# Four of eight K-tile pairs of the FFN inputs by Strassen's scheme, with two sets of blocks for their sums and two sums formed by accumulating DMA

## The chip, the core and the metric

The kernel runs on one core of one Trainium2 chip. The core has a matrix engine (TensorE, in the profile PE, with its weight loads as PEld), VectorE (DVE), ScalarE (ACT), GpSimd (POOL) and SyncE (SP); 128 partitions of on-chip memory (SBUF); a matrix accumulator (PSUM) of eight banks; and 16 DMA engines that move data between device memory (HBM) and SBUF. Each engine works through its own queue in order and waits on semaphores. The metric is the device time of one execution in microseconds; less is better.

## The reference

One layer of a streaming encoder on 256 tokens of width 2048, all in float32. Cut to what matters here:

```python
def swiglu_ffn(x, w_in, w_out):
    g, u = jnp.split(x @ w_in, 2, axis=-1)
    return (jax.nn.silu(g) * u) @ w_out
...
        h = layer_norm(ALPHA * h + 0.5 * swiglu_ffn(h, ffn1_w_in[l], ffn1_w_out[l]), ln_ffn1_g[l], ln_ffn1_b[l])
        mix = hybrid_mixer(h, w_in[l], gate_bias[l], rel_bias[l], q_a_norm[l], w_q_b[l], kv_a_norm[l],
                           w_kv_b[l], w_o_a[l], w_o_b[l], w_out[l], cos, sin)
        h = layer_norm(ALPHA * h + mix, ln_mix_g[l], ln_mix_b[l])
        xa = memory_cross_attention(h, mem, mem_ln_g[l], mem_ln_b[l], w_xq[l], w_xkv[l], w_xo[l])
        h = layer_norm(ALPHA * h + xa, ln_x_g[l], ln_x_b[l])
        h = layer_norm(ALPHA * h + 0.5 * swiglu_ffn(h, ffn2_w_in[l], ffn2_w_out[l]), ln_ffn2_g[l], ln_ffn2_b[l])
```

The change touches the product `x @ w_in` of both FFNs: (256 x 2048) by (2048 x 11008), where 5504 columns are the gate g and 5504 the "up" half u.

## The kernel before

**Halves.** A float32 product is made of three products of a shorter format (float32r). Every operand v is kept as a high half (v rounded, a copy by ScalarE) and a low half (v minus the high half, a subtraction by VectorE). A product of x and w is x_hi w_hi + x_hi w_lo + x_lo w_hi: three matmuls, "passes", into one bank. `split` (L244, L245) makes both halves; `run` does the same for weights in L213 and L216.

**Weights.** All weights stream from HBM as tiles of 128 x 2048 into `raw` (three buffers, DMAs issued by SP in L175), and their halves go into units of 128 x 1024 (`unit`, four buffers each for high and low halves). `run` walks through a list of items, each with its weights, and emits the loading of the next item's weights (`load`, at most four units in use) ahead of the item's matmuls. Each item may have a priority. A framework then orders the instructions of every engine's queue and sets the semaphores.

**The FFN's input.** The 5504 gate and up columns are taken in groups of 512 (`in_group`, j = 0 to 9, and a rest of 384, j = 10). A group needs four banks: two token halves (tt) by gate and up (g). Its K dimension of 2048 is 16 tiles of 128, taken as eight pairs k; each pair is one weight tile of 1 MiB. A plain pair (`mm_pair`, L296) issues 2 tiles x 2 x 2 x 3 = 24 matmuls of 512 columns. Group 0 of FFN 1 stands in `start`, and group 0 of FFN 2 in `first_group`. The hidden columns are processed in three parts (`F_SPLIT`: groups 0 to 2, 3 to 6, 7 to 10); after each part its output product (`out_proj`, L285) follows, four columns of the output by three or four weight tiles.

**Strassen's scheme.** Seen as a 2 x 2 by 2 x 2 block product (two K tiles, two token halves, gate and up), a pair can be computed with seven block products rather than eight: 21 matmuls (`mm_sums`, L340). In groups 1 to 9 the pairs in `SUMS_AT` (k = 2, 4, 6) are done so. The sums on the activations' side are made once per FFN (`sum_forms`, L311 to L317, into blocks X0, X1). The sums on the weights' side are made for each such pair from the raw tile (`form_sums`, L183): three additions on VectorE into a block H5 (one of 1024 columns, two of 512), then the halves of the two sums of 1024 columns each, into blocks that rotate over X2, X3 and H4. Beside them the pair's plain blocks are split (1024 and 512 columns). Four products go to a second set of four banks (`qs`), which serve as the next group's banks afterwards; `shared` (L568 to L573) takes them out after the last Strassen pair, and `product` in `hidden` (L614 to L617) adds them to the group's banks. `turn` transposes the gated result (L629) into the blocks H0 to H3; in the middle of a part it runs inside the next group, between its second and third pair.

**Order of emission.** In `load(i)`: fetch tile i, form the sums of tile i and tile i + 1 if they are Strassen pairs, then split tile i.

## Time and profile before

| | us |
|---|---|
| median of 3 runs (2529.89 to 2531.62) | 2531.01 |
| the profiled execution | 2530.41 |
| its span, first to last instruction | 2528.6 |

The page of the profile gives the busy time of each engine over the span; the chain that ended last, followed back from the last instruction to what released each step; groups of instructions by source line (L296 is line 296); and the DMA queues. A row of a group names the operation, output and inputs by the program's names, the shape, the count, then busy time, mean ns of one, and the idle time in front of them with what ended it. Windows give the busy time of each engine in a stretch of the span. Matmuls overlap in their pipeline, so a single one is listed with 389 ns while the next starts before it ends.

### The profile page before, as it was taken

To read this page: it belongs to the slowest core of one execution; us is meant where nothing else is said; L and a number is where in the kernel's file an instruction comes from. 1 tells how busy PE (TensorE), PEld (TensorE's weight loads), DVE (VectorE), ACT (ScalarE), POOL (GpSimd) and SP (SyncE) were. 2 spreads that over 40 slices of the span, in tenths; PEclk is the share of its full clock that TensorE was granted. 3 is DMA by queue.
4 is the path that set the end of the run, shared out by engine and by line. 5 is a ranking of instruction groups with operands and counts; after the bars stand their busy time and mean duration, and the time that the engine had idled before them with its cause. 6 is when DMAs were issued, how large, how long until landed. Compare 5 with 4: busy or idle time off the path is not lost.

```text
span 2528.6 us, 32077 instructions
## 1 busy us (share of the span) xinstructions
PE 2512.6 (99%) x12590; PEld 2123.7 (84%) x12590; DVE 1808.0 (72%) x2420; ACT 1279.3 (51%) x1734; POOL 30.0 (1%) x87
## 2 busy tenths in 40 slices
PE   9999999999999999999999999999999999999998
PEld 8888888889888888888888888888888888888896
DVE  6967985796666776755558784555878788758856
ACT  5545553554444555544445554454555455445543
POOL 0000000000000000000000000000000000000000
PEclk9999999999999999999999999999999999999999
DMA  7655655555645644555457565544555655555563
GB/s 259 243 186 183 216 193 192 198 200 191 227 155 185 201 143 142 183 192 183 175 192 261 188 217 194 189 163 138 200 181 202 211 205 183 203 197 200 183 231 136
DMA packets 74040, 488.04 MB, mean 193 GB/s; under 512 B 8609, under 2 KB 8865, under 8 KB 20769
## 3 DMA queue, kind: packets, MB, share of 16 engines
q1 hardware_dynamic: 69216, 468.18, 52.9%
q0 software_dynamic: 3808, 15.73, 2.0%
q8 instruction: 98, 1.61, 0.2%
q10 hardware_dynamic: 864, 2.10, 0.2%
q14 instruction: 54, 0.43, 0.1%
HBM read 482.69 MB, written 2.10 MB: 192 GB/s over the span
## 4 chain that ended last, share of the span: by engine, by line
PE 96%; DVE 2%; DMA 1%; ACT 0%; issue 0%; DVEq 0%; ACTq 0%
PE mm L285 31%; PE mm L265 17%; PE mm L296 13%; PE at L296 10%; PE mm L266 8%; PE mm L340 5%; PE at L340 5%; PE mm L254 2%; DMA raw<-ffn_w_in 1%; PE at L717 1%; DVE lo L216 0%; PE at L1152 0%; PE at L1130 0%; PE at L863 0%; PE at L391 0%; PE at L928 0%
## 5 line engine op out<-in xcount | busy, mean ns | idle before, releaser
L216 DVE TENSOR_TENSOR lo<-raw,hi 128x1024 fp32r<-128x1024 f32 (+1 forms) x742 | 893.7, 1208 | 576.1 <-ACT hi L213 561.5
L213 ACT CAST hi<-raw 128x1024 fp32r<-128x1024 f32 (+1 forms) x742 | 769.9, 1039 | 917.5 <-PE mm L285 369.1
L285 PE MATMUL mm<-hi,H 128*128 128x512 f32 x1640 | 508.7, 389 | 0.0
L265 PE MATMUL mm<-T,hi 128*128 128x512 f32 x1168 | 415.3, 399 | 0.0
L285 PEld LDWEIGHTS mm<-hi,H 128*128 128x128 f32 x1640 | 307.9, 188 | 63.4
L266 PE MATMUL mm<-T,lo 128*128 128x256 f32 x1168 | 328.2, 281 | 0.0
L285 PE MATMUL mm<-lo,H 128*128 128x512 f32 x820 | 319.2, 389 | 0.0
L296 PE MATMUL mm<-hi,T 128*128 128x512 f32 (+1 forms) x1024 | 308.7, 376 | 0.4 <-ACT hi L244 0.4
L265 PEld LDWEIGHTS mm<-T,hi 128*128 128x128 f32 x1168 | 219.5, 188 | 54.3 <-issue 1.2
L296 PE MATMUL at<-hi,T 128*128 128x512 f32 x800 | 253.0, 389 | 0.0
L265 PE MATMUL mm<-H,hi 128*128 128x512 f32 x640 | 225.9, 397 | 0.0
L266 PEld LDWEIGHTS mm<-T,lo 128*128 128x128 f32 x1168 | 220.6, 189 | 0.1
L296 PEld LDWEIGHTS mm<-hi,T 128*128 128x128 f32 x1024 | 190.4, 188 | 31.1 <-ACT hi L244 1.4
L296 PE MATMUL mm<-lo,T 128*128 128x512 f32 (+1 forms) x512 | 193.1, 377 | 0.2 <-DVE lo L245 0.2
L285 PEld LDWEIGHTS mm<-lo,H 128*128 128x128 f32 x820 | 154.0, 188 | 31.9 <-DVE lo L216 0.2
L266 PE MATMUL mm<-H,lo 128*128 128x256 f32 x640 | 179.0, 280 | 0.0
L296 PEld LDWEIGHTS at<-hi,T 128*128 128x128 f32 x800 | 150.2, 188 | 31.2
L296 PE MATMUL at<-lo,T 128*128 128x512 f32 x400 | 156.1, 390 | 0.0
L265 PEld LDWEIGHTS mm<-H,hi 128*128 128x128 f32 x640 | 120.2, 188 | 29.0
L285 PE MATMUL mm<-hi,X 128*128 128x512 f32 x416 | 130.0, 390 | 0.0
L245 DVE TENSOR_TENSOR lo<-raw,hi 128x1024 fp32r<-128x1024 f32 (+1 forms) x126 | 119.2, 975 | 10.3 <-ACT hi L244 10.1
L244 ACT CAST hi<-raw 128x1024 fp32r<-128x1024 f32 (+1 forms) x126 | 103.7, 853 | 44.3 <-PE mm L296 13.3
(242 smaller groups left out, 3181.7 us busy)
## 6 DMA issues: line engine op xcount, KB each, us to landing
raw<-ffn_w_in SPq DMA_DIRECT2D x151, 1024.0 KB, 4.8
raw<-ffn_w_out SPq DMA_DIRECT2D x80, 1024.0 KB, 4.8
raw<-w_gate SPq DMA_DIRECT2D x32, 1024.0 KB, 4.8
raw<-w_qk SPq DMA_DIRECT2D x16, 1024.0 KB, 4.8
raw<-w_o_b SPq DMA_DIRECT2D x16, 1024.0 KB, 4.8
raw<-w_out SPq DMA_DIRECT2D x16, 1024.0 KB, 4.9
raw<-w_xk SPq DMA_DIRECT2D x16, 1024.0 KB, 4.8
raw<-w_xv SPq DMA_DIRECT2D x16, 1024.0 KB, 4.9
```

The lines of the kernel that those rows point to most:

```text
L213: self.nc.scalar.copy(hi[:, :m], raw[:, c:c + m])
L216: self.nc.vector.tensor_tensor(lo[:, :m], raw[:, c:c + m], hi[:, :m].bitcast(F32), ALU.subtract)
L244: self.nc.scalar.copy(hi, src)
L245: self.nc.vector.tensor_tensor(lo, src, hi.bitcast(F32), ALU.subtract)
L254: self.nc.tensor.matmul(ps, w[u][wi][:, c:c + P], x.at(xi, kt), start=(j == 0 and k == 0), stop=(j == n - 1 and k == 2),)
L265: self.nc.tensor.matmul(ps, hi, x.both(kt), start=(kt == 0), stop=False)
L266: self.last_mm = self.nc.tensor.matmul(ps[:, :S], lo, x.at(0, kt), start=False, stop=(kt == n - 1))
L285: self.last_mm = self.nc.tensor.matmul(ps, x.at(xi, kt)[:, tt * P:(tt + 1) * P], w[u][wi][:, c:c + 512], start=(start and j == 0 and k == ...
L296: self.last_mm = self.nc.tensor.matmul(ps[tt, g][:, :n], x.at(xi, kt)[:, tt * P:(tt + 1) * P], hi_lo[wi][:, g * n:(g + 1) * n], start=(kt ...
L340: self.last_mm = self.nc.tensor.matmul(bank, a[xi], hi_lo[wi][:, c:c + 512], start=own and first and j == 0, stop=own and last and j == 2)
L717: self.nc.tensor.transpose(ps[:, i * P:(i + 1) * P], s[:, c:c + P], self.ident)
```

## The change

- `SUMS_AT` goes from (2, 4, 6) to (2, 3, 5, 6): four pairs of each group of 512 go by Strassen's scheme. The layout of the weights in HBM swaps gate and up in both K tiles of such a pair, so that the three plain blocks lie side by side.
- The two blocks of sums on the weights' side each have a whole set for high and low halves: (X2, X3) and (H4, H5), used in turn.
- For the first two Strassen pairs of a group (`ADDED`), the first sum of 1024 columns is not made by VectorE. GpSimd copies 1024 columns from HBM into a buffer Y0 or Y1 and then adds 512 columns, twice, in a second, accumulating DMA from HBM. It is emitted up to four items ahead. VectorE makes the other two sums of 512 from it (into Y2). In the other two pairs VectorE makes all three.
- The units for weight halves become two rings (`place`) of 4 x 1024 columns; weights of the FFN inputs get one subtraction for their whole low half (2048, or 1536 in a Strassen pair).
- In `mm_pair` and `mm_sums` all matmuls with high halves of the weights come first, then those with low halves.
- In `load(i)` the split of tile i comes ahead of the sums.
- The scratch space for GpSimd's DMA descriptors is set to 4096 bytes.

```diff
--- before.py
+++ after.py
@@ -23,8 +23,9 @@
 NF = D_FF // P
 NG = D_FF // 512
 F_SPLIT = (12, 16, 15)
-SUMS_AT = (2, 4, 6)
-SUM_TAGS = ("X2", "X3", "H4")
+SUMS_AT = (2, 3, 5, 6)
+ADDED = (0, 1)
+SETS = (("X2", "X3"), ("H4", "H5"))
 A_HEADS, A_DIM = 16, 64
 B_HEADS, NOPE, ROPE, V_DIM = 16, 128, 64, 128
 X_HEADS, X_DIM = 4, 512
...
@@ -102,6 +102,8 @@
         self.uid = 0
         self.chain = None
         self.turns = 0
+        self.cur = 0
+        self.ring = [self.halves.tile([P, UNITS * 1024], F32R, name=f"ring{i}") for i in range(2)]
 
 
     def name(self, s):
@@ -166,7 +168,7 @@
                 return 2
             return 0 if w[1] else -(-w[0].shape[1] // 1024)
 
-        raws, sums = {}, {}
+        raws, sums, adds = {}, {}, {}
 
         def fetch(i):
             if i not in raws:
@@ -175,46 +177,72 @@
                 self.last_load = self.nc.sync.dma_start(raws[i][:, :ap.shape[1]], ap)
             return raws[i]
 
+        def four(ap, a=4):
+            return ap.rearrange("p (a n) -> p a n", a=a)
+
+        def begin_sums(i):
+            ap, k = queue[i].ap, self.turns % 2
+            self.turns += 1
+            t = self.block(f"Y{k}", (P, 1024))
+            adds[i] = t, k
+            if queue[i].added:
+                self.nc.gpsimd.dma_start(t, ap[:, 512:1536])
+                self.nc.gpsimd.dma_start(four(t, 2), four(ap)[:, 0:1].to_broadcast([P, 2, 512]), accum_op=ALU.add)
+
         def form_sums(i):
-            raw, t = fetch(i), self.block("H5", (P, 2048))
-            for a, b, c in ((slice(0, 1024), raw[:, 0:1024], raw[:, 512:1536]),
-                            (slice(1024, 1536), t[:, 0:512], raw[:, 1024:1536]),
-                            (slice(1536, 2048), t[:, 1024:1536], raw[:, 1536:2048])):
-                self.nc.vector.tensor_tensor(t[:, a], b, c, ALU.add)
-            sums[i] = []
-            for k in range(2):
-                blk = self.block(SUM_TAGS[self.turns % len(SUM_TAGS)], (P, 2, 1024), F32R)
-                self.turns += 1
-                self.split(t[:, k * 1024:(k + 1) * 1024], blk[:, 0, :], blk[:, 1, :])
-                sums[i].append((blk[:, 0, :], blk[:, 1, :]))
+            r = four(fetch(i))
+            if i not in adds:
+                begin_sums(i)
+            (t, k), u = adds[i], self.block("Y2", (P, 1024))
+            if not queue[i].added:
+                self.nc.vector.tensor_tensor(four(t, 2), r[:, 1:3], r[:, 0:1].to_broadcast([P, 2, 512]), ALU.add)
+            for out, a, b in ((u[:, :512], t[:, :512], 2), (u[:, 512:], u[:, :512], 3)):
+                self.nc.vector.tensor_tensor(out, a, r[:, b], ALU.add)
+            hi, lo = (self.block(g, (P, 2048), F32R) for g in SETS[k])
+            for src, c in ((t, 0), (u, 1024)):
+                self.split(src, hi[:, c:c + 1024], lo[:, c:c + 1024])
+            sums[i] = [(four(hi)[:, a], four(lo)[:, a]) for a in range(4)]
 
         def load(i):
             w = queue[i]
             raw = fetch(i)
+            for k in range(i, min(i + 5, len(queue))):
+                if isinstance(queue[k], Sums) and queue[k].added and k not in adds:
+                    begin_sums(k)
+            got = split_own(i, w, raw)
 
             for k in (i, i + 1):
                 if k < len(queue) and isinstance(queue[k], Sums) and k not in sums:
                     form_sums(k)
-            got = []
+            return got + sums[i] if isinstance(w, Sums) else got
+
+        def split_own(i, w, raw):
             if isinstance(w, Sums):
-                for a, b in ((1024, 2048), (0, 512)):
-                    hi, lo = self.unit()
-                    self.split(raw[:, a:b], hi[:, :b - a], lo[:, :b - a])
-                    got.append((hi, lo))
-                return got + sums[i]
+                hi, lo = self.place(1536)
+                for a, b in ((0, 512), (512, 1536)):
+                    self.nc.scalar.copy(hi[:, a:b], raw[:, 512 + a:512 + b])
+                self.nc.vector.tensor_tensor(lo, raw[:, 512:], hi.bitcast(F32), ALU.subtract)
+                return [(hi[:, c:c + 512], lo[:, c:c + 512]) for c in (0, 512, 1024)]
             ap, tags = w
             n = ap.shape[1]
+            step = 768 if ap.tensor.name.endswith("_w_in_r") else 1024
             if tags:
-                blk = [self.block(g, (P, 2048), F32R) for g in tags[:2]]
-            step = 768 if ap.tensor.name.endswith("_w_in_r") else 1024
+                hi, lo = [self.block(g, (P, 2048), F32R) for g in tags[:2]]
+            elif "_w_in" in ap.tensor.name:
+                hi, lo = self.place(n)
+                for c in range(0, n, step):
+                    self.nc.scalar.copy(hi[:, c:c + step], raw[:, c:c + step])
+                self.nc.vector.tensor_tensor(lo, raw[:, :n], hi.bitcast(F32), ALU.subtract)
+                return [(hi[:, c:c + step], lo[:, c:c + step]) for c in range(0, n, step)]
+            got = []
             for c in range(0, n, step):
                 m = min(step, n - c)
-                hi, lo = [x[:, c:c + step] for x in blk] if tags else self.unit()
-                self.nc.scalar.copy(hi[:, :m], raw[:, c:c + m])
+                h, l = [x[:, c:c + m] for x in (hi, lo)] if tags else self.place(m)
+                self.nc.scalar.copy(h, raw[:, c:c + m])
 
                 with self.tc.issue_after(self.chain.ins) if self.chain is not None else nullcontext():
-                    self.nc.vector.tensor_tensor(lo[:, :m], raw[:, c:c + m], hi[:, :m].bitcast(F32), ALU.subtract)
-                got.append((hi, lo))
+                    self.nc.vector.tensor_tensor(l, raw[:, c:c + m], h.bitcast(F32), ALU.subtract)
+                got.append((h, l))
             return got
 
         def early(w):
@@ -289,15 +317,16 @@
 
     def mm_pair(self, ps, w, n, x, kts):
 
-        for (hi_lo, kt) in zip(w, kts):
-            for tt in range(2):
-                for g in range(2):
-                    for k, (wi, xi) in enumerate(((0, 0), (1, 0), (0, 1))):
-                        self.last_mm = self.nc.tensor.matmul(
-                            ps[tt, g][:, :n], x.at(xi, kt)[:, tt * P:(tt + 1) * P],
-                            hi_lo[wi][:, g * n:(g + 1) * n],
-                            start=(kt == 0 and k == 0), stop=(kt == KT - 1 and k == 2),
-                        )
+        for passes in (((0, 0), (0, 1)), ((1, 0),)):
+            for (hi_lo, kt) in zip(w, kts):
+                for tt in range(2):
+                    for g in range(2):
+                        for wi, xi in passes:
+                            self.last_mm = self.nc.tensor.matmul(
+                                ps[tt, g][:, :n], x.at(xi, kt)[:, tt * P:(tt + 1) * P],
+                                hi_lo[wi][:, g * n:(g + 1) * n],
+                                start=(kt == 0 and wi + xi == 0), stop=(kt == KT - 1 and wi == 1),
+                            )
 
     def sum_forms(self, x):
 
@@ -321,25 +350,22 @@
 
 
         k = 2 * SUMS_AT[i]
-        u1, u2, t13, t24 = w
+        r0, r2, r3, t0, t1, t2, t3 = w
 
         def plain(kt, tt):
             return [x.at(a, kt)[:, tt * P:(tt + 1) * P] for a in (0, 1)]
 
         n5, s2, n3, s3 = ([forms[i][:, a, j, :] for a in (0, 1)] for j in range(4))
         first, last = i == 0, i == len(SUMS_AT) - 1
-        for bank, a, (hi_lo, c), own in (
-                (ps[0, 0], plain(k + 1, 0), (u1, 512), False),
-                (ps[0, 1], n3, (u1, 0), False),
-                (qs[0], plain(k, 0), (u2, 0), True),
-                (qs[1], n5, (t13, 0), True),
-                (qs[3], s3, (t13, 512), True),
-                (qs[2], s2, (t24, 0), True),
-                (ps[1, 0], plain(k + 1, 1), (t24, 512), False)):
-            for j, (wi, xi) in enumerate(((0, 0), (1, 0), (0, 1))):
-                self.last_mm = self.nc.tensor.matmul(
-                    bank, a[xi], hi_lo[wi][:, c:c + 512],
-                    start=own and first and j == 0, stop=own and last and j == 2)
+        parts = ((ps[0, 0], plain(k + 1, 0), r3, False), (ps[0, 1], n3, r2, False), (qs[0], plain(k, 0), r0, True),
+                 (qs[1], n5, t0, True), (qs[3], s3, t1, True), (qs[2], s2, t2, True),
+                 (ps[1, 0], plain(k + 1, 1), t3, False))
+        for passes in (((0, 0), (0, 1)), ((1, 0),)):
+            for bank, a, hi_lo, own in parts:
+                for wi, xi in passes:
+                    self.last_mm = self.nc.tensor.matmul(
+                        bank, a[xi], hi_lo[wi],
+                        start=own and first and wi + xi == 0, stop=own and last and wi == 1)
 
 
     def rsqrt(self, v, y, a):
...
@@ -493,9 +519,11 @@
     def raw_tile(self):
         return self.wraw.tile([P, 2048], F32, tag="raw", name=self.name("raw"))
 
-    def unit(self):
-        return (self.whi.tile([P, 1024], F32R, tag="hi", name=self.name("hi")),
-                self.wlo.tile([P, 1024], F32R, tag="lo", name=self.name("lo")))
+    def place(self, n):
+        c, k = self.cur, -(-n // 1024)
+        assert c + k <= UNITS
+        self.cur = (c + k) % UNITS
+        return [r[:, c * 1024:c * 1024 + n] for r in self.ring]
 
 
     def ffn(self, tag, xT, st, first=None, steps=None, late=None, before=None, tags=None):
@@ -550,7 +578,7 @@
                     if i == 0:
                         qs.update((a, self.group_tile(j + 1)) for a in range(4))
                     self.mm_sums(ps, qs, w, xT(), self.forms, i)
-                self.add(fn, Sums(ap))
+                self.add(fn, Sums(ap, i in ADDED))
                 if i == len(SUMS_AT) - 1:
                     self.add(lambda: self.shared(qs), prio=SOON)
                 continue
@@ -1249,7 +1277,7 @@
     w = np.stack([m.reshape(k // P, P, c // n, n) for m in (u, g)])
     if n == 512:
         for i in SUMS_AT:
-            w[:, 2 * i + 1, :, 1:] = w[::-1, 2 * i + 1, :, 1:].copy()
+            w[:, 2 * i:2 * i + 2, :, 1:] = w[::-1, 2 * i:2 * i + 2, :, 1:].copy()
     return w.transpose(3, 2, 1, 0, 4).reshape(c // n, P, k // P * 2 * n)
 
 
@@ -1314,7 +1342,7 @@
     from concourse.bass_utils import run_bass_kernel_spmd
 
     arrays = _layout(inputs)
-    nc = bacc.Bacc("TRN2", target_bir_lowering=False, num_devices=1)
+    nc = bacc.Bacc("TRN2", target_bir_lowering=False, num_devices=1, dynamic_dma_scratch_size=4096)
     t = {
         k: nc.dram_tensor(k, v.shape, mybir.dt.from_np(v.dtype), kind="ExternalInput").ap()
         for k, v in arrays.items()
```

In `start` the two units of a pair become one `place(2048)`, split in the same steps as before.

More of the change, by code (lines that the diff above doesn't have):

```diff
@@ L75, with __init__ @@
 class Sums:
-    def __init__(self, ap):
-        self.ap = ap
+    def __init__(self, ap, added):
+        self.ap, self.added = ap, added
 class Kernel:
@@ L92, in __init__ @@
         self.wraw = pool("wraw", 3)
-        self.whi = pool("whi", UNITS)
-        self.wlo = pool("wlo", UNITS)
+        self.halves = pool("halves")
         self.blocks = pool("blocks")
@@ L476, in start @@
             self.split(v, xT.blk(0, 2 * k, 2), xT.blk(1, 2 * k, 2))
-            w = [self.unit() for _ in range(2)]
-            for c in range(2):
-                for d in range(0, 1024, 512 if k == 0 else 1024):
-                    e = d + (512 if k == 0 else 1024)
-                    self.split(raw[:, c * 1024 + d:c * 1024 + e], w[c][0][:, d:e], w[c][1][:, d:e])
+            hi, lo = self.place(2048)
+            for c in range(0, 2048, 512 if k == 0 else 1024):
+                e = c + (512 if k == 0 else 1024)
+                self.split(raw[:, c:e], hi[:, c:e], lo[:, c:e])
+            w = [(hi[:, c:c + 1024], lo[:, c:c + 1024]) for c in (0, 1024)]
             self.mm_pair(ps, w, 512, xT, (2 * k, 2 * k + 1))
```

## The prediction

> **What bounds the kernel now.** The page comes first: span, engines, chain of work that ended last.
>
> ```profile
> span 2528.6 us, 32077 instructions
> PE 2512.6 (99%) x12590; PEld 2123.7 (84%) x12590; DVE 1808.0 (72%) x2420; ACT 1279.3 (51%) x1734; POOL 30.0 (1%) x87
> PE 96%; DVE 2%; DMA 1%; ACT 0%; issue 0%; DVEq 0%; ACTq 0%
> ```
>
> TensorE is busy 99% of the span and makes 96% of the chain: a matmul less is worth its own time wherever nothing else ends later. The 72% of VectorE is an average over unequal stages, so next come the windows of three input groups of FFN 1 (group 1, then the first and second of the next half), with the columns window; its length and the busy time of TensorE, of weight loads, VectorE, ScalarE and GpSimd; clock, DMA share, GB/s.
>
> ```profile
> 51.41:93.98 42.57, 42.57 (x193) 35.06 (x192) 40.89 (x57) 25.20 (x31) 0.00 (x0) 1.00 0.61 220
> 202.79:244.27 41.48, 41.48 (x185) 34.36 (x184) 33.99 (x37) 22.29 (x26) 0.00 (x0) 1.00 0.61 212
> 244.27:286.89 42.62, 42.62 (x193) 35.07 (x192) 38.29 (x44) 24.17 (x29) 0.00 (x0) 1.00 0.57 198
> ```
>
> TensorE has no idle time in any of them, at full clock. But VectorE works 38.29 of 42.62 us in an ordinary group and 40.89 of 42.57 in group 1. It is the engine that can become the bound here. In the ordinary group its idle time was mostly this (window 244.27 to 286.89, waits of VectorE; total, times, longest):
>
> ```profile
> DVE lo L216 <- ACT hi L213: 3.7, 4, 1.5
> ```
>
> These are weight halves whose ring slot TensorE had not freed yet: VectorE was ahead, not late. Over the whole run TensorE waited for a Strassen block hardly at all:
>
> ```profile
> PE mm L340 <- DVE H L245: 1.3, 1, 1.3
> ```
>
> **The matmuls removed.** The chain around two pairs of group 3 (start, us, what):
>
> ```profile
> 218.43 5.44 PE at L296 x24
> 223.87 1.36 PE at L340 x6
> 225.23 2.72 PE mm L340 x12
> 227.95 0.68 PE at L340 x3
> 228.63 5.44 PE at L296 x24
> ```
>
> A plain pair is 24 matmuls in 5.44 us, a Strassen pair 6+12+3 = 21 in 228.63 - 223.87 = 4.76. Both give 0.227 us a matmul and follow each other without a gap. So a conversion saves 0.68 us. The number of conversions comes from the first addition of each Strassen pair:
>
> ```profile
> L183 DVE TENSOR_TENSOR H<-raw 128x1024 f32<-128x1024 f32 x54 | 65.8, 1219 | 11.5 <-DMA raw<-ffn_w_in 11.5
> ```
>
> 54 = 2 FFNs x 9 groups x 3. Four per group makes 72, 18 more: 18 x 0.68 = **-12.2 us**, if TensorE stays fed. The order inside a pair (high halves first) changes no count; the bank changes as often in L340 as it will, at the same 0.227, so I price the order at 0.
>
> **VectorE's account in a group.** It pipelines, so what counts is start to start (start, duration):
>
> ```profile
> 247.32 0.69 DVE L183 TENSOR_TENSOR H<-H,raw 128x512 f32<-128x512 f32 x1
> 247.92 1.22 DVE L245 TENSOR_TENSOR X<-H,X 128x1024 fp32r<-128x1024 f32 x1
> 249.06 1.22 DVE L216 TENSOR_TENSOR lo<-raw,hi 128x1024 fp32r<-128x1024 f32 x1
> 250.19 1.22 DVE L245 TENSOR_TENSOR X<-H,X 128x1024 fp32r<-128x1024 f32 x1
> ```
>
> 512 columns take 0.60, 1024 take 1.14. That is 0.54 per 512 plus 0.06 fixed, which gives estimates of 1.68 for 1536 and 2.21 for 2048. Plain pair: before 2 x 1.14 = 2.28, after one instruction of 2.21. Strassen pair before: additions 1.14 + 2 x 0.60, four low halves 3 x 1.14 + 0.60: 6.36. After: own half 1.68, two sums' low halves 2.28, additions 2 x 0.60 where DMA made the first sum (5.16) and 1.14 more where not (6.30). Group before: 5 x 2.28 + 3 x 6.36 = 30.5; after: 4 x 2.21 + 2 x 5.16 + 2 x 6.30 = 31.8. So +1.3: 38.29 becomes **39.6 of 42.62 - 0.68 = 41.94 us**, 94% where it was 90%; 2.3 us a group may stay idle. A broadcast input is taken at the price of a plain one (no row shows it; bounds 0 and, if each 512 were its own instruction, 0.06 more).
>
> Is it in time? The order of emission is: pair i+1's own low half (it waits until pair i-1 has left TensorE), then the sums of pair i+2. Behind these waits VectorE's queue holds only work for later pairs. By pair time on TensorE I let VectorE's backlog run. Beside pair 0: products of the last group 6 x 0.60 = 3.6, half 2.2, sums of pair 2 3.5, together 9.3 against 5.44, 3.9 left over. Beside pair 1: 1.7 + 3.5, left 3.6. Pair 2 (with the transposes' splits, 1.2, and 1.1 us of transposes): left 0.6. Pair 3: 2.2 + 4.6 against 4.76, left 2.7. Pair 4: 1.7 + 4.6, left 3.5. Pairs 5 to 7 are light and clear it. The sums of a pair are due two pairs (10.2 to 10.9 us) and six matmuls, which need no sum (1.4 us), after their turn comes, their low halves two thirds into the pair; the worst are done after 9.3 and 9.0. Nothing is late, with 2.5 us to spare. ScalarE has 24.17 of 42.62 and gains one sum's copies (about 2): hidden behind its idle 18.
>
> Group 1 of FFN 1 is the exception. A further form of the activations has to be made there, from these rows:
>
> ```profile
> 58.79 0.69 DVE L311 TENSOR_TENSOR w<-T 128x512 f32<-128x512 f32 x1
> 59.39 0.29 DVE L315 TENSOR_TENSOR w<-w,w 128x128 f32<-128x128 f32 x1
> 59.59 0.69 DVE L245 TENSOR_TENSOR lo<-raw,hi 128x512 fp32r<-128x512 f32 x1
> ```
>
> 0.60 + 4 x 0.20 + a split of 0.60 = 2.0. So 40.89 + 1.3 + 2.0 = 44.2 us against 41.9, and the second Strassen pair is now due one pair earlier. The excess is 2.3; group 2 has room for what is not due at once. Bounds 0 and 2.3; I take **+1.0**, near the middle as part of it is due later. In FFN 2 the forms come beside earlier work of the group's own gate and up matmuls: 0. There stands the one wait of 1.3 us quoted above; it may go or stay, 0 with bounds -1.3 and +1.3.
>
> **Start.** The first pair waits for its second K tile:
>
> ```profile
> 9.82 0.50 PE L296 MATMUL mm<-hi,T 128*128 128x512 f32 x1 [0.22 <-ACT hi L244]
> 10.55 40.87 PE mm L296 x179
> ```
>
> Before, 12 matmuls were over when that tile came and 179 followed without a gap from 10.55. After, only the 8 of the high half can run ahead, so 184 are left at about 9.9: 9.9 + 184 x 0.227 = 51.7 against 51.42. **+0.2**.
>
> **The accumulating DMAs** are the operation that the trace doesn't have. Per group GpSimd issues two plain copies of 512 KB and two accumulations of 512 KB, each accumulation after its copy has landed. Nearest rows (KB, median us from issue to landing):
>
> ```profile
> raw<-ffn_w_in SPq DMA_DIRECT2D x151, 1024.0 KB, 4.8
> raw<-w_va SPq DMA_DIRECT2D x8, 1024.0 KB, 6.8
> w<-gb POOLq DMA_DIRECT2D x24, 256.0 KB, 4.3
> T<-mem POOLq DMA_DIRECT2D x2, 1024.0 KB, 6.2
> ```
>
> A copy of 512 KB lies between 4.3 and 6.2; I take 4.9. An accumulation reads its target as well: 4.3 at least, 2 x 6.2 = 12.4 at most; I take 6.2, the row with as many bytes read. Buffer Y0 comes free some 2.7 us into pair 4; its next sum is due at the next group's pair 2, less 2.6 for additions and copies: 2.7 + 4.8 + 4.8 + 5.4 + 6.5 + 5.4 - 2.6 = 27 us later. Y1's is due a pair after, at 33. The chain on GpSimd is 4.9 + 2 x A, as the second copy runs beside the first accumulation: 17.3 at A = 6.2, 29.7 at 12.4, both under 33. In front of FFN groups its queue has nothing else; the gain loads of FFN 2 (w<-gb) stand behind it, beside output matmuls that have slack. Cost **0**; bounds 0 and the rival below.
>
> Do they slow the weight loads? Eight loads took a DMA share of 0.57 x 42.62 = 24.3 us of all engines; with two MiB more, the accumulations counted twice, 24.3 x 11/8 = 33.4 of 41.9, or 0.80. A load of 6.8 in place of 4.8 would still be early: a raw buffer is refilled when its pair's low half is made, and its data is due two pairs later. So 0.
>
> **Sum.** 2530.4 for the profiled execution (span 2528.6 and 1.8 around it) - 12.2 + 1.0 + 0.2 = 2519.4; the runs' median, 2531.0, lies 0.6 above that execution: **2520 us**, own range 2516.5 to 2523.
>
> **Rivals.**
> 1. *VectorE becomes the bound.* For it: 94% with an order full of waits. Against: the idle time before was waiting for slots, not lateness. If half of what it loses today beyond 2.3 us stays (idle 42.62 - 38.29 = 4.3, so 3.3), a group lasts 39.6 + 3.3 = 42.9, 0.3 over today: 18 x 0.3, **2536**. At 4.3 it is 18 x 1.3: 2554. It eats gain from 2.3 idle and decides the sign at 3.0; half of its chance lies within 0.2%.
> 2. *The accumulation comes too late; slower.* Place: the form of the sums on VectorE, then TensorE. 4.9 + 2A passes 33 us at A = 14. Groups that follow another input group at once, 6 per FFN, pay: at A = 16, 3.9 x 12 = 47 less 12: **2566**. Against it: 16 us is over twice the row for as many bytes. Slower by 5 us from A = 14.8.
> 3. *The transfers run one after another.* Ten MiB a group at 4.8 us each are 48 us, not 41.9: 18 x 6.1 = 110 worse, **2630**. Against it: eight loads at 4.8 would fill 38.4 us of a group, yet their share is 24.3, so transfers overlap already. The Trainium skill is on its side in part: "DMA: Bandwidth & Descriptors", "Issuing engines are not separate DMA queues", says that transfers of every issuing engine run on the same 16 DMA engines and interleave, so a second queue gains only issue time. No run here yet shows both queues full.
> 4. *The change doesn't do what it says*: TensorE takes longer per matmul in the new order, or waits for high halves, by 0.5 us a group: 2520 + 9 = **2529**. The rows of L340, which already mix banks and operands at 0.227, speak against it.
>
> **Chances.** Forecast 0.66; rival 1 0.18 (0.08 of it within 0.2%, 0.10 slower); rival 2 0.08; rival 3 0.02; rival 4 0.06, within. A measurement of this kernel tells about 0.2%, 5 us, from no change. Faster 0.66, same 0.14, slower 0.20. The range of 8 in 10 takes the forecast, rival 4 and the lower part of rival 1: 2516.5 to 2535.
>
> **What would show it.** TensorE's count falls by 54; an ordinary group lasts 41.94 us with VectorE at 39.6 and TensorE without idle time. Strassen matmuls waiting for a block's high half from ScalarE, with VectorE over 41, mean rival 1. VectorE's half-sum additions waiting for a GpSimd DMA, with landings of accumulations over 14 us, mean rival 2. Group 1 of FFN 1 should lose about 1 us. Most easily wrong: A, which no row shows, and group 1.

## The result, and the profile after

| | us |
|---|---|
| median before (4 runs, 2529.89 to 2531.62) | 2531.09 |
| median after (4 runs, 2683.05 to 2698.63) | 2696.55 |
| ratio, 95% interval | 1.0643, 1.0623 to 1.0663 |
| the profiled execution of after, its span | 2683.05, 2681.0 |

The kernel became 6.4% slower; 2520 had been forecast. The profiled execution is the shortest of the four, 13.5 us under their median, so the terms that are read from its trace below are a little small. The page of the changed kernel shows this in the lines that were read before:

```profile
span 2681.0 us, 32104 instructions
PE 2542.4 (95%) x12536; PEld 2138.1 (80%) x12536; DVE 1833.2 (68%) x2326; ACT 1302.2 (49%) x1772; POOL 93.6 (3%) x159
PEclk9999988999999999999999999999998998899999
q0 software_dynamic: 18784, 53.48, 8.1%
PE 72%; issue 10%; DVE 8%; DMA 8%; ACT 1%; POOL 1%; ACTq 0%; DVEq 0%; POOLq 0%
```

TensorE issues 54 matmuls fewer (12536), as forecast, yet it is busy 29.8 us longer and idle 2681.0 - 2542.4 = 138.6 us, where it was idle 16.0. The granted clock falls below full in the slices of the FFN inputs. The chain, 96% TensorE before, now goes through VectorE, DMAs and waiting. VectorE is busy 68%, where it was 72%; that it is not the bound (rival 1) is settled by the first experiment.

Lines of the changed kernel: L189 is the copy and L190 the accumulation that GpSimd issues; L272 and L273 are the two halves of a `split`; L596 to L601 are `shared`, which empties the Strassen banks; L642 to L645 are the product of gate and up; L325 is a plain pair, L366 a Strassen pair, L313 the output product. The view of waits, engine by engine (total us, times, longest):

```profile
POOL Y L189 <- DVE X L273: 1265.9, 17, 388.8
POOL Y L190 <- DMA Y<-ffn_w_in: 177.5, 30, 9.8
...
ACT H L272 <- DMA Y<-ffn_w_in: 156.3, 17, 12.5
...
DVE w L598 <- ACT w L596: 116.9, 14, 10.7
...
PE mm L313 <- DVE w L642: 35.2, 3, 12.2
PE mm L325 <- ACT w L596: 26.5, 7, 6.4
PE at L325 <- ACT w L596: 19.3, 4, 6.7
```

Read from the bottom: TensorE waits for `shared` (L596, by ScalarE) and for the product (L642, by VectorE). VectorE's part of `shared` waits for ScalarE's (116.9 us). ScalarE stands 156.3 us in front of a high half of a block H made from Y, waiting for a DMA. GpSimd's 1265.9 us are mostly idle time in which nobody needs it; what they say is that a copy starts when VectorE's L273 has read the buffer for the last time.

The timeline of one group boundary shows the order in ScalarE's queue (start, duration, engine, line, operation, count; in brackets the idle time before it and what ended it):

```profile
298.76 0.59 POOL L189 DMA_DIRECT2D Y<-ffn_w_in  x1 [30.61 <-DVE X L273]
303.12 1.18 POOL L190 DMA_DIRECT2D Y<-ffn_w_in  x1 [3.76 <-DMA Y<-ffn_w_in]
306.75 0.60 POOL L189 DMA_DIRECT2D Y<-ffn_w_in  x1 [2.45 <-DVE H L273]
312.34 1.18 POOL L190 DMA_DIRECT2D Y<-ffn_w_in  x1 [5.00 <-DMA Y<-ffn_w_in]
...
323.18 1.04 ACT L272 CAST H<-Y 128x1024 fp32r<-128x1024 f32 x1 [9.51 <-DMA Y<-ffn_w_in]
324.13 0.58 ACT L596 COPY w<-at 128x512 f32<-128x512 f32 x1
...
324.76 2.90 PE L325 MATMUL at<-ring,T 128*128 128x512 f32 x6 [4.39 <-ACT w L596]
...
345.02 0.62 PE L366 MATMUL at<-ring,T 128*128 128x512 f32 x2
```

At 306.75 buffer Y1 is free and its copy goes out; the accumulation follows at 312.34, and ScalarE can read the sum at 323.18. That sum is for the next group's second Strassen pair. Directly behind it in ScalarE's in-order queue stands L596 for the group that is ending, and the next group's first matmuls wait for the banks that L596 empties. A transfer that nobody needs before pair 3 thus stops pair 0: TensorE was idle for 4.39 us up to 324.76. Pairs 0 and 1 end at 338.84, then come transposes and pair 2; pair 3 begins at 345.02 (the last line), some 22 us after its sum had come.

The stops also cost clock. Four windows of after (columns as in the prediction):

```profile
381.00:394.00 13.00, 13.00 (x51) 10.57 (x51) 11.12 (x13) 5.30 (x7) 0.00 (x0) 0.80 0.45 162
394.00:436.50 42.50, 30.30 (x134) 24.53 (x133) 29.87 (x29) 19.52 (x24) 3.55 (x4) 0.89 0.65 198
436.50:450.00 13.50, 13.49 (x53) 10.99 (x54) 6.94 (x9) 4.53 (x6) 0.00 (x0) 0.84 0.40 135
460.00:530.00 70.00, 70.00 (x311) 57.96 (x310) 36.94 (x34) 28.90 (x28) 0.00 (x0) 1.00 0.56 193
```

In the first and the third, TensorE has work throughout, but the clock is 0.80 and 0.84 and a matmul takes 13.00 / 51 = 0.255 us; in the undisturbed stretch it is 70.00 / 311 = 0.225. The Trainium skill states the rule in "TensorE: Matmul & The Clock Gate", "Why this matters for your kernels": no idle gap of TensorE over some 3 us between bursts, or the clock falls back to half. The trace agrees: TensorE's stop of 2.04 us up to 278.47 left the clock at 1.00 (256 to 300 us), while after the stop of 6.38 us that ended at 376.72 it was 0.56 from 381 to 387 and 1.00 again from 387 to 394.

### The profile page after: what moved, and what is told of

The parts are those of the page before. It is cut to its first block, busy times and chain, and to the rows that moved or that the text cites. A ratio compares the mean times of both kernels' runs of the same rounds, so it can differ in the third digit from the quotient of the medians.

```text
span 2681.0 us, 32104 instructions
## 1 busy us (share of the span) xinstructions
PE 2542.4 (95%) x12536; PEld 2138.1 (80%) x12536; DVE 1833.2 (68%) x2326; ACT 1302.2 (49%) x1772; POOL 93.6 (3%) x159
## 4 chain that ended last, share of the span: by engine, by line
PE 72%; issue 10%; DVE 8%; DMA 8%; ACT 1%; POOL 1%; ACTq 0%; DVEq 0%; POOLq 0%
PE mm L313 30%; PE mm L293 15%; PE mm L294 8%; DMA Y<-ffn_w_in 6%; PE mm L325 6%; PE at L325 4%; PE mm L282 2%; PE at L366 2%; PE mm L366 2%; DVE ring L224 1%; DVE H L273 1%; DVE X L273 1%; DVE Y L200 1%; DVE ring L235 1%; POOL Y L190 1%
## 5 line engine op out<-in xcount | busy, mean ns | idle before, releaser
L244 DVE TENSOR_TENSOR ring<-raw,ring 128x1024 fp32r<-128x1024 f32 (+1 forms) x530 | 642.9, 1217 | 466.9 <-ACT ring L241 450.3
L241 ACT CAST ring<-raw 128x1024 fp32r<-128x1024 f32 (+1 forms) x530 | 551.9, 1046 | 633.0 <-PE mm L313 368.8
L313 PE MATMUL mm<-ring,H 128*128 128x512 f32 x2460 | 570.8, 394 | 42.6 <-DVE w L642 35.2
L313 PEld LDWEIGHTS mm<-ring,H 128*128 128x128 f32 x2460 | 466.7, 190 | 142.1 <-issue 36.3
L293 PE MATMUL mm<-T,ring 128*128 128x512 f32 x1168 | 412.0, 396 | 0.0
L325 PE MATMUL mm<-ring,T 128*128 128x512 f32 (+1 forms) x1344 | 312.5, 392 | 46.3 <-ACT w L596 26.5
L325 PEld LDWEIGHTS mm<-ring,T 128*128 128x128 f32 x1344 | 258.2, 198 | 96.9 <-ACT w L596 29.4
L294 PE MATMUL mm<-T,ring 128*128 128x256 f32 x1168 | 327.8, 281 | 0.0
L293 PEld LDWEIGHTS mm<-T,ring 128*128 128x128 f32 x1168 | 219.1, 188 | 51.4 <-issue 1.0
L325 PE MATMUL at<-ring,T 128*128 128x512 f32 x960 | 236.5, 405 | 24.6 <-ACT w L596 19.3
L325 PEld LDWEIGHTS at<-ring,T 128*128 128x128 f32 x960 | 187.8, 197 | 69.0 <-ACT w L596 21.0
L294 PEld LDWEIGHTS mm<-T,ring 128*128 128x128 f32 x1168 | 220.6, 189 | 0.1
L234 ACT CAST ring<-raw 128x1024 fp32r<-128x1024 f32 (+1 forms) x176 | 172.1, 1013 | 92.7 <-PE mm L313 31.8
L272 ACT CAST H<-Y 128x1024 fp32r<-128x1024 f32 x72 | 75.0, 1048 | 180.4 <-DMA Y<-ffn_w_in 156.3
L313 PE MATMUL mm<-ring,X 128*128 128x512 f32 x624 | 143.5, 390 | 0.0
L313 PEld LDWEIGHTS mm<-ring,X 128*128 128x128 f32 x624 | 116.7, 188 | 24.2 <-issue 0.2
```

Of the source, the lines that this page charges most:

```text
L234: self.nc.scalar.copy(hi[:, c:c + step], raw[:, c:c + step])
L241: self.nc.scalar.copy(h, raw[:, c:c + m])
L244: self.nc.vector.tensor_tensor(l, raw[:, c:c + m], h.bitcast(F32), ALU.subtract)
L272: self.nc.scalar.copy(hi, src)
L293: self.nc.tensor.matmul(ps, hi, x.both(kt), start=(kt == 0), stop=False)
L294: self.last_mm = self.nc.tensor.matmul(ps[:, :S], lo, x.at(0, kt), start=False, stop=(kt == n - 1))
```

## The experiments

Each run is compared with the kernel before on the same chip, since its median is not the same in every series of runs (2524 to 2531 us). Diffs are against the changed kernel unless said otherwise. A second measure is used as well: the profiled span less the mixer between the FFNs, because the same kernel's mixer is 6 us longer in some executions than in others (below, under the repeat of the kernel before). It runs from 96 matmuls that stand alone to an output product of 264; in the chain of the first experiment below (start, duration):

```profile
837.29 11.50 PE mm L282 x96
...
1366.96 59.88 PE mm L313 x264
```

| kernel | span | mixer | span without it |
|---|---|---|---|
| before, first profile | 2528.6 | 535.1 | 1993.5 |
| before, again | 2523.7 | 529.4 | 1994.3 |
| after | 2681.0 | 530.2 | 2150.8 |
| all sums on VectorE | 2517.7 | 529.7 | 1988.0 |
| two DMA sums, own buffers and order | 2533.6 | 529.3 | 2004.3 |
| one DMA sum, the same | 2527.6 | 536.1 | 1991.5 |
| three pairs, no DMA sums | 2529.1 | 529.1 | 2000.0 |
| the same, old order of passes | 2528.1 | 535.1 | 1993.0 |
| all sums on VectorE, forms early | 2516.9 | 530.1 | 1986.8 |
| four pairs, forms early, old order of passes | 2508.6 | 530.1 | 1978.5 |

**All sums on VectorE.**

```diff
-ADDED = (0, 1)
+ADDED = ()
```

> VectorE makes the first sum of all four Strassen pairs; no accumulating DMA is left, all else is as changed. Theory A (sums made by DMA come late, and their copies stand in ScalarE's queue ahead of the copies that free the next group's banks): the waits go, 2515 to 2530 us, no ScalarE wait for a DMA into Y. Theory B (the fourth Strassen pair, the rings or the new order starve TensorE, VectorE being the bound): stays above 2600. Theory C (two more MiB a group crowd out the weight loads): as A here.

Measured: 2521.68 us, ratio 0.9989 (0.9980 to 0.9998), TensorE idle for 20.6 us. Everything that the change loses hangs on the accumulating DMAs: theory B is out, while A and C expected the same here. That 2521.68 lies near the forecast of 2520 is chance; the forecast was 11.0 us below the kernel before, and this run is 2.6 below it. Against this run, after is 2681.0 - 2517.7 = 163.3 us longer in span: 138.6 - 20.6 = 118.0 of idle time and 2542.4 - 2497.1 = 45.3 of slower matmuls. The window of an ordinary group of this run:

```profile
245.80:287.85 42.05, 42.05 (x190) 34.53 (x189) 40.66 (x41) 24.47 (x29) 0.00 (x0) 1.00 0.54 197
```

42.05 us with VectorE at 40.66, making all four sums where the change makes two: forecast were 41.94 and (39.6 + 2 x 1.14) 41.9. In this group VectorE at 97% still doesn't hold TensorE up.

**Only the order of the queues.** The work that reads an accumulated sum is ordered behind the last product on ScalarE and VectorE; buffers and transfers stay.

```diff
-                    nc.scalar.activation(s[tt], s[tt], AF.Silu)
-                    nc.vector.scalar_tensor_tensor(s[tt], up, 0.5, s[tt], ALU.mult, ALU.mult)
+                    self.silu = nc.scalar.activation(s[tt], s[tt], AF.Silu)
+                    self.done = nc.vector.scalar_tensor_tensor(s[tt], up, 0.5, s[tt], ALU.mult, ALU.mult)
...
+            late = queue[i].added and self.done is not None
+            with self.tc.issue_after(self.done.ins) if late else nullcontext():
+                with self.tc.issue_after(self.silu.ins) if late else nullcontext():
                     for out, a, b in ((u[:, :512], t[:, :512], 2), (u[:, 512:], u[:, :512], 3)):
```

> The DMAs stay as changed. Only the order on ScalarE and VectorE differs: all work on the sums that DMA has a part in is queued behind the last group's gating. Theory A: most of the loss goes, 2520 to 2560 us; what is left is TensorE waiting for the sums themselves. Theories B and C: no less than 2650.

Measured: 2549.79 us, ratio 1.0103 (1.0086 to 1.0120), clock 0.998. Its accumulations land no sooner (median 7.6 us, at most 15.0, as in after), and yet most of the loss is gone, as theory A had it. So the same transfer times cost little when nothing urgent stands behind the wait for them.

**Only the buffers.** Y0 and Y1 for the accumulated sums alone, a third buffer for VectorE's; the order is not touched. Its space comes from one work buffer and the DMA scratch.

```diff
-            t = self.block(f"Y{k}", (P, 1024))
+            t = self.block(f"Y{k}" if queue[i].added else "Y3", (P, 1024))
...
-        return self.work.tile(list(shape), dt, tag="w1", bufs=6, name=self.name("w1"))
+        return self.work.tile(list(shape), dt, tag="w1", bufs=5, name=self.name("w1"))
```

> The two buffers that DMA fills are kept to themselves (VectorE's own first sums go to a third buffer; room for it from one temporary of the mixer and the descriptor scratch), so GpSimd may start as soon as the last DMA-made sum is used, some 25 us earlier in a group. Queue orders are left to themselves. Theory A1, the late start is the cause: the sums are there in time, the waits go, and what is left is the price of the transfers, 3 to 15 us above e1_vector_all. Theory A2, the queue order alone: no less than 2600.

Measured: 2540.53 us, ratio 1.0066 (1.0050 to 1.0083). ScalarE then waits for an accumulating DMA once, for 4.9 us. An earlier start alone cures the wait as well: either remedy takes away most of the loss, so the loss needs both the late start and the order. By the two ratios this run lies 19 us above the kernel with all sums on VectorE, where 3 to 15 were expected.

**Both.** 

> Both: own buffers for the DMA-made sums and their work queued behind the last group's gating. By A1 and A2 alike 3 to 15 us above e1_vector_all, 10 to 20 below e3_after_product; if it stays at e3_after_product, the transfers' contention is what is left, not the start.

Measured: 2536.93 us, ratio 1.0046 (1.0031 to 1.0061). This still lies 14 to 16 us above the kernel without accumulating DMAs. Where it comes from is shown in the DMA issues of the all-VectorE kernel and of this one (KB each, median us to landing):

```profile
raw<-ffn_w_in SPq DMA_DIRECT2D x151, 1024.0 KB, 4.7
```

```profile
raw<-ffn_w_in SPq DMA_DIRECT2D x151, 1024.0 KB, 5.7
```

and in the waits of VectorE in this one:

```profile
DVE Y L199 <- DMA raw<-ffn_w_in: 19.0, 6, 4.4
...
DVE Y L205 <- DMA raw<-ffn_w_in: 10.7, 6, 2.8
```

The weight tiles come a microsecond later, and the sums wait for them. The chain of this run that ended last stops for weight tiles in both FFNs; the longest of these stops:

```profile
1869.66 9.74 DMA raw<-ffn_w_in
```

**The transfers without their sums.** VectorE makes all sums, and the same 72 transfers go to a buffer that nothing reads.

```diff
+                    z, ap = self.block("Y1", (P, 1024)), queue[k].ap
+                    self.nc.gpsimd.dma_start(z, ap[:, 512:1536])
+                    self.nc.gpsimd.dma_start(four(z, 2), four(ap)[:, 0:1].to_broadcast([P, 2, 512]), accum_op=ALU.add)
```

> VectorE makes all sums, as in e1_vector_all (from one buffer for the first sum, not two), but GpSimd issues the same copies and accumulations into a buffer that nothing reads. Theory A: within 5 us of e1_vector_all, as nothing waits for them. Theory C: 20 us or more above e1_vector_all, with weight loads that land in over 6 us and waits for raw tiles.

Measured: 2535.44 us, ratio 1.0046 (1.0031 to 1.0061): 13.8 us over the kernel without the transfers on the same chip. Theory A expected 5 at most and theory C 20 or more, so neither was right. Nothing held GpSimd back here: all 36 chains were issued between 1.8 and 501 us, one after another, some 13.9 us each, and the loss is all in FFN 1. VectorE's first sums share a single buffer in this run; that is not the cause, since FFN 2, with the same buffer and no transfers beside it, takes no longer (from the mixer's end 1150.8 us, 1150.7 with all sums on VectorE). The chain that ended last has stops for weight tiles in FFN 1, after the start this as the longest:

```profile
244.59 7.89 DMA raw<-ffn_w_in
```

and the window of that stretch shows the DMA engines at 0.79:

```profile
100.00:700.00 600.00, 590.99 (x2666) 490.38 (x2665) 472.12 (x456) 307.97 (x351) 51.06 (x58) 1.00 0.79 251
```

So the transfers alone cost about what both remedies together leave, though not in the same place: here all of it in FFN 1, there 5.6 us in FFN 1 and 10.7 in FFN 2. The prediction cited the Trainium skill, "DMA: Bandwidth & Descriptors", "Issuing engines are not separate DMA queues": the traces agree that GpSimd's transfers slow SP's. They don't run one after another, though: the 110 us of rival 3 are 14 to 16.

**A copy in place of the addition.**

```diff
-                self.nc.gpsimd.dma_start(four(t, 2), four(ap)[:, 0:1].to_broadcast([P, 2, 512]), accum_op=ALU.add)
+                self.nc.gpsimd.dma_start(four(t, 2), four(ap)[:, 0:1].to_broadcast([P, 2, 512]))
```

> The second DMA overwrites where it should add, so the first sum of two Strassen pairs a group is left out; every transfer, wait and queue order otherwise stays. If the accumulation itself is slow (7.6 us median from issue to landing, up to 14.8), it lands in about 5 us and the time falls to 2580 to 2640 us. If the chain of two dependent transfers and its late start are the cost, whatever the second one does, it stays within 20 us of 2696.

Measured: 2602.95 us, ratio 1.0314 (1.0282 to 1.0345), within the range for a slow accumulation, though the transfer did not get as short as expected. The second transfer lands after 6.6 us in the median and 9.0 at most, against 7.6 and 14.8 with the addition; the view of after's line L190 has:

```profile
L190 POOL DMA_DIRECT2D Y<-ffn_w_in x36: 1170/1184/1235, 12.8 to 2491.3; - x36
...
DMA to landing us min/median/max: 5.9/7.6/14.8
```

GpSimd takes 1184 ns to issue the accumulation, 712 the copy. That a chain shorter by 1.5 us in the median (1.0 in landing, 0.5 in issue) halves the loss shows how steeply it grows once the wait begins: ScalarE's wait falls from 156.3 to 78.6 us, and the clock stays at 0.988 where after had 0.972.

**One accumulated sum instead of two**, with its own buffer and ordered (`ADDED = (0,)` and the edits of "both").

> One sum a group by accumulating DMA instead of two, with a buffer of its own, and the work that reads it ordered behind the product of the group before. Half the extra transfers, no late start and nothing queued behind the wait. Theory (what is left of the loss with own buffers and order is the load of the transfers on the weight loads, in proportion to their bytes): half of the 14 us by which two sums lie above none, so about 7 us over the variant with all sums on VectorE: ratio 1.0015 to 1.003 to the kernel before. Rival 1 (the load costs something only when the DMA engines are nearly full, so half is hidden): 0.999 to 1.0005. Rival 2 (what is left is a chain that is late, one sum being as late as two): 1.004 to 1.005.

Measured: 2529.02 us, ratio 1.0000 (0.9990 to 1.0011), with executions of both lengths of the mixer in it. Without the mixer its span is 1991.5 us, against 1988.0 for none and 2004.3 for two: the first sum costs 3.5 us, the second 12.8. The cost of the transfers is not in proportion to their bytes, and the ratio is within rival 1's range. The DMA engines' share from 100 to 700 us is 0.57, 0.65 and 0.70 with none, one and two sums, which fits a load that costs only when the engines are well filled. This share is not the whole account: two sums cost FFN 1 5.6 us at 0.70 and FFN 2 10.7 at 0.68 (1900 to 2500 us), and why FFN 2 loses more was not found.

**Three Strassen pairs, no accumulating DMA**: what the new order and rings cost by themselves.

```diff
-SUMS_AT = (2, 3, 5, 6)
-ADDED = (0, 1)
+SUMS_AT = (2, 4, 6)
+ADDED = ()
```

> Three Strassen pairs (2, 4, 6) as before the change, no accumulating DMA; the rings, the single low half of 2048, the two sets and the order high halves first stay as changed. If these cost nothing by themselves: the time of the kernel before, within 4 us. If they are what eats the 12 us that e1_vector_all did not gain: 6 us or more above the kernel before.

Measured: 2531.27 us, ratio 1.0024 (1.0015 to 1.0034), 6.2 us over the kernel before. I had priced these parts at about nothing. The next five runs look for the cause.

**The forms of FFN 1 during group 0** (on the all-VectorE kernel): the activations' forms of group 1 are made after pairs 3 to 6 of group 0.

```diff
+            if k == 0:
+                self.forms = []
+            if 3 <= k <= 6:
+                self.forms += self.sum_forms(xT, k - 3)
```

> e1_vector_all (all sums by VectorE), and the forms of the activations in FFN 1 made during group 0, one after each of the pairs 3 to 6, where VectorE has 3 us idle per pair, and not in group 1. If VectorE's excess in group 1 costs what the trace of e1_vector_all suggests (some 3.5 us), it is 2 to 4 us below e1_vector_all; if the loss lies elsewhere, no change.

Measured: 2520.32 us, ratio 0.9981 (0.9972 to 0.9991). The first output product of FFN 1 starts at 146.41 us instead of 147.87: 1.5 us gained in the first groups, where 2 to 4 were expected. Without the mixer the whole span is 1.2 shorter (1986.8 against 1988.0).

**Low halves in two pieces** (on that kernel).

```diff
-                    self.nc.scalar.copy(hi[:, c:c + step], raw[:, c:c + step])
-                self.nc.vector.tensor_tensor(lo, raw[:, :n], hi.bitcast(F32), ALU.subtract)
+                    self.split(raw[:, c:c + step], hi[:, c:c + step], lo[:, c:c + step])
```

> All sums on VectorE, the forms of the activations made during group 0, and the low half of a plain pair of the FFN input made by two subtractions of 1024 columns rather than one of 2048 (in a Strassen pair it stays one). Theory (one long subtraction keeps later work of VectorE's queue waiting for a whole ring slot, so pieces help): 1 to 2 us less than the same kernel with one subtraction, ratio 0.9975 or lower. Rival (the fixed 0.06 us of the second instruction is all that changes, and it is hidden): 0.998 as without, within 0.0007.

Measured: 2525.20 us, ratio 0.9987 (0.9977 to 0.9996). Without the mixer (535.8 of 2524.2) the span is 1988.4, against 1986.8 with one subtraction. No gain: the length of the subtraction isn't the cause.

**Sums ahead of the split again** (on the forms-early kernel; the two blocks in `load` change places).

> All sums on VectorE and the forms made during group 0, as in the best variant so far (0.9981), but in load the sums of tiles i and i + 1 are again emitted ahead of the split of tile i, as in the kernel before. Theory (of the 6 us that the new order and rings cost with three Strassen pairs, the order of emission in load is the cause): 3 to 6 us less than that variant, ratio 0.9957 to 0.997. Rival (the order of the passes or the rings are the cause): 0.998 again, or more where the own split now comes late for a Strassen pair, 1.000 to 1.004.

Measured: 2520.75 us, ratio 0.9988 (0.9979 to 0.9997). No gain: the order of emission isn't the cause either.

**Passes in the old order** (on the forms-early kernel).

```diff
-        for passes in (((0, 0), (0, 1)), ((1, 0),)):
+        for passes in (((0, 0), (1, 0), (0, 1)),):
```

> The same variant (0.9981), but the three passes of a block product follow each other again, high by high, low by high, high by low, as in the kernel before. Theory (passes with the low halves last give VectorE a third of a pair more time for them, which is needed): low halves come late, TensorE waits for VectorE, 1.000 or more. Rival (the order of passes costs the start, since only 8 rather than 12 matmuls can run before the second K tile has come, and little else): up to 2 us less than that variant, 0.997 to 0.998.

Measured: 2510.71 us, ratio 0.9947 (0.9933 to 0.9960), the fastest of all, 14.1 us below the kernel before. The order of the passes costs 14.1 - 4.7 = 9.4 us by the medians and 1986.8 - 1978.5 = 8.3 by the spans without the mixer, against both theories, the rival's 2 us too. The timelines at the end of a part show one place. With low halves last:

```profile
134.00 0.69 DVE L607 TENSOR_TENSOR w<-w,at 128x512 f32<-128x512 f32 x1
134.60 0.68 DVE L608 TENSOR_TENSOR w<-w,at 128x512 f32<-128x512 f32 x1
135.21 1.23 DVE L244 TENSOR_TENSOR ring<-raw,ring 128x1024 fp32r<-128x1024 f32 x1
136.35 0.68 DVE L649 TENSOR_TENSOR w<-w,mm 128x512 f32<-128x512 f32 x1
...
137.08 8.46 PE L313 MATMUL mm<-ring,H 128*128 128x512 f32 x36 [1.07 <-DVE w L649]
```

and with each block's three passes together:

```profile
133.08 0.69 DVE L650 TENSOR_TENSOR w<-w,mm 128x512 f32<-128x512 f32 x1
...
134.92 8.33 PE L313 MATMUL mm<-ring,H 128*128 128x512 f32 x36
```

With the old order a bank of the last pair is complete nine matmuls before the pair ends (three passes for each of the other three banks), so the product (L649, L650) can begin while TensorE still works, and the output product follows without a gap. With low halves last, all four banks are complete only in the last four matmuls; a ring split (L244) stands ahead of the product, and TensorE waits. More is in the middle groups, by the windows of the same group without and with the edit:

```profile
244.35:286.40 42.05, 42.05 (x190) 34.53 (x189) 40.65 (x41) 24.47 (x29) 0.00 (x0) 1.00 0.54 196
```

```profile
242.06:283.78 41.72, 41.72 (x189) 34.61 (x189) 41.25 (x41) 25.13 (x30) 0.00 (x0) 1.00 0.57 201
```

That is 0.33 us. By the chains of the two runs groups 1, 4, 5, 8 and 9 of FFN 1 are 0.27 to 0.33 us shorter each, while groups 3 and 7, which hold no transposes, take 40.80 us in both; the rest is at the start and at the ends of the parts. Why a group with transposes gains was not found. Over the run TensorE's busy time falls by 2496.9 - 2492.9 = 4.0.

**Three pairs with the passes in the old order.** 

> Three Strassen pairs, all sums on VectorE, as in the run that lay 6.2 us above the kernel before, but with the passes of a block product in the old order. What is then left of the change are the two rings, the emission of the own split ahead of the sums, and the long low halves. Theory (the order of the passes cost the 6.2 us, and also what the four-pair kernel gained when it was undone): 0.998 to 1.000, that is 2520 to 2525 us. Rival (the gain from undoing it needs four pairs, and the rings or the emission cost the 6 us here): 1.0015 or more.

Measured: 2529.98 us, ratio 1.0009 (0.9998 to 1.0020). The ratio mixes two lengths: nine of its 12 times lie at 2529.8 to 2530.9 and three at 2523.6 to 2526.0, while 13 of the 17 of before lie at 2523.4 to 2525.9. Without the mixer the span is 1993.0, against 2000.0 with low halves last and 1994.3 for the kernel before: by the spans the passes cost 7.0 us, all of the 6 that were looked for, and rings and emission cost nothing that shows here. The ratio alone lies between the ranges of the theory and the rival.

**The kernel before again.** 

> The kernel before, unchanged, profiled on this chip, so that its stages can be laid beside those of the variants run here. Question: the mixer, from the first of its 96 matmuls to its output, took 535.1 us in the first profile of this kernel and 529 to 530 us in every variant, which all have the weight halves in two rings. Theory (the rings or the order made the mixer faster): 535 us here again. Rival (a difference between chips): 529 to 530 us here too. Total 2524 to 2531 us by either.

Measured: 2525.44 us; the mixer takes 1367.62 - 838.24 = 529.4 us, where the first profile had 535.1. It is the same kernel, so neither the rings nor the order made it faster. The groups of TensorE by form differ at L265, in the first profile and in this one:

```profile
L265 PE MATMUL mm<-T,hi 128*128 128x512 f32 x1168 | 415.3, 399 | 0.0
...
L265 PE MATMUL mm<-H,hi 128*128 128x512 f32 x640 | 225.9, 397 | 0.0
```

```profile
L265 PE MATMUL mm<-T,hi 128*128 128x512 f32 x1168 | 412.1, 396 | 0.0
...
L265 PE MATMUL mm<-H,hi 128*128 128x512 f32 x640 | 223.3, 393 | 0.0
```

The two rows differ by 5.8 us together, as much as the mixer does. A difference between chips isn't the cause either: the runs of the kernel before on this one chip have totals at 2523 to 2527 and at 2530 to 2533 us. Profiles of changed kernels show both lengths. What sets them wasn't found.

## Why the prediction was wrong

- **Matmuls removed: right.** 54 fewer, and a Strassen pair takes 4.76 us where the clock is full (groups 3 and 7 without the accumulating DMAs, 40.80 us, are 4 x 5.44 + 4 x 4.76). With the old passes, the forms early and all sums on VectorE the kernel gains 14.1 us, a little more than the 12.2 for the matmuls; where the rest comes from was not looked into.
- **VectorE's account: right.** 40.66 us of a 42.05 us group with all four sums, 1.2 less than the account gives, and TensorE doesn't wait there. Rival 1 did not happen, even with 2.28 us more than the change gives VectorE.
- **The accumulating DMA, priced at 0: the step that failed.** The time of a transfer was only a little off (A of 6.2 forecast, 7.6 in the median, within the bounds of 4.3 and 12.4; the longest, 14.8, lies above them), and the chain meets its due times of 27 and 33 us: in the boundary shown, Y0's copy goes out at 298.76 and the second sum has come 24.4 us later. What failed is the sentence on ScalarE: "gains one sum's copies (about 2): hidden behind its idle 18". The 2 us are hidden, but the first of these copies waits for the DMA, and what stands behind it in the queue is due some 20 us before the sum is. I wrote down what is queued behind VectorE's waits and did not do it for ScalarE. Rival 2 had the right kind, a wait for the accumulation, in the wrong place and with the wrong condition: it was to stand on VectorE and begin at A = 14, and it stood on ScalarE at a median of 7.6. Size: 2150.8 us without the mixer against 2004.3 with own buffers and order, 146.5 us, of it 2542.4 - 2499.7 = 42.7 in matmuls that took longer, at a mean clock of 0.972 instead of 0.997.
- **The load of the transfers, priced at 0: wrong by 14 to 16 us.** The share of the DMA engines was foreseen (0.80 forecast, 0.70 over the FFN with own buffers and order, 0.79 with unpaced transfers). That a load of 6.8 us would "still be early" did not hold: at a median of 5.7 the sums already waited.
- **The order of the passes, priced at 0: wrong by 7 to 9 us.** I counted matmuls and bank changes and did not ask when each bank is complete.
- **Group 1 of FFN 1 and the start: right in kind, somewhat low.** +1.0 and +0.2 were forecast. With all sums on VectorE the first output product starts at 147.87 us against 145.66, +2.2 although two groups had become faster by 2 x 0.68: 3.6 lost. The early forms gave back 1.5 of it (146.41), which is group 1's part. The old order of the passes gave back 2.3 more (144.12), the start's part among them: group 1 began at 51.98 us with all sums on VectorE and at 51.41 in the kernel before, +0.6.

The terms add up, in spans without the mixer: before 1993.5; after 2150.8, that is +157.3. Of these 146.5 are the queue and the late start, which the runs can't divide since either remedy removes most of it; 2004.3 - 1988.0 = 16.3 are the transfers' load; and 1988.0 - 1993.5 = -5.5 is the rest of the change, where -11.0 was forecast. The order of the passes, 7 to 9 us, is more than that difference.

## What to carry to other kernels

When work is moved to a DMA, list for every engine that reads its result what stands behind that first read in the in-order queue, and when that is due; the slack of the result itself says nothing. A transfer can be early enough for its reader and still stop the kernel. And when the passes of an accumulation are reordered, ask when each bank is complete, not only how many matmuls there are.

## What the runs showed of the hardware

- After idle gaps of 4.39 and 6.38 us in TensorE's work the granted clock was 0.60 (324.7 to 329 us) and 0.56 (381 to 387); a gap of 2.04 us left it at 1.00. Against all sums on VectorE the matmuls of the whole run took 45 us longer, beside 118 us more of waiting.
- An accumulating DMA of 512 KB in SBUF lands 7.6 us after its issue (5.9 to 14.8) where a copy in the same place takes 6.6 (4.0 to 9.0), and GpSimd is busy 1184 ns with its issue, against 712.
- Additional transfers did not cost in proportion to their bytes: 18.9 MB cost 3.5 us, 37.8 MB 16.3, with the DMA engines' share over the first FFN at 0.65 and 0.70 where it was 0.57 without them.
- The same kernel has two lengths of the mixer, 529 and 535 us, with a mean of 396 or 399 ns a matmul in one row of L265 and 393 or 397 in another.
